# Additions in DRAM in four pieces each, and a fixed order of splits in the first channel block of a ConvFFN

## The chip, the cores and the metric

The kernel runs on one core of a Trainium2 chip. A core has a matrix engine (TensorE, PE in the profile, with its weight loads as PEld), three engines for elementwise work (VectorE or DVE, ScalarE or ACT, GpSimd or POOL), and SyncE (SP), which here only issues transfers. Transfers run on 16 DMA engines that all queues share; a queue of SP and a queue of POOL feed them in this kernel. The metric is the device time of one execution in microseconds (us). Before the change, three runs gave 1703.12, 1707.95 and 1720.14 us, so the median is 1707.95 us.

## What is computed

One layer of a diffusion backbone is applied to 128 context tokens and 1024 latent tokens of width 1024: a mixer of gated linear attention, then a channel mixer, each with a normalisation and a modulation before it and a gate behind it. The change lies in the channel mixer:

```python
def dw_conv(u, conv_w, conv_b, grid):
    # 3x3 over the latent grid (16 rows of 64), width 3 over the context tokens
    ...
    return out + conv_b

def conv_ffn(h, w_up, conv_w, conv_b, w_down, grid):
    u = dw_conv(h @ w_up, conv_w, conv_b, grid)
    gate, up = jnp.split(u, 2, axis=-1)
    return (jax.nn.silu(gate) * up) @ w_down

# in trunk_layer
h = rmsnorm(x, norm2) * (1 + scale2) + shift2
x = x + gate2 * conv_ffn(h, w_ffn_up, ffn_conv, b_ffn_conv, w_ffn_down, grid)
```

Everything is float32. `w_ffn_up` is 1024 x 5632 and `w_ffn_down` 2816 x 1024.

## The kernel before

**Products in float32.** PE multiplies a rounded form of float32 here. Each operand is therefore split into a high part, which ACT copies into the rounded type, and a low part, which DVE or POOL computes as the difference (`split_lo`, line 62). A product is three matmul passes: high x high, high x low, low x high.

**Seven products in place of eight.** The up projection and the down projection both use a Strassen-like scheme. Tokens and inner dimension are halved, sums and differences of the halves of both operands are formed, and seven products of half size replace eight. For the up projection the token operands are `b11`, `b21`, `b22`, straight from the normalised tokens, and the sums `t1` to `t4`; the weight operands are the blocks `11`, `12`, `21`, `22` of a channel's columns and the sums `s1` to `s4`. The 128 context tokens have an operand `p` of their own.

**The up stage.** It has 22 channel blocks (`c` from 0 to 21, called channels below) of 128 gate and 128 up columns. In channel `c` PE runs the products in an order that is written out (`chained`): for every channel but the first 5 (`t1`), the transposed context columns of the channel before (`prompt_columns`, line 1507), product 4 of the channel before (`t4`), 2 (`b21`), 3 (`b22`), 1 (`b11`), the context product's first half, 6 (`t2`), its second half, 7 (`t3`). Channel 0 begins with 1, 2, 5 and has 6, 3 and then both halves of the context product. DVE adds partial products (lines 1572, 1573, 1579) and runs the 3x3 convolution as eight multiply-adds over each half (`conv_rows`, line 1426), after ACT has written the middle tap (line 1414). The result of the gate half and of the up half are multiplied on POOL (line 1522) and stored to DRAM (`scr_g`, line 1523). Every second channel POOL forms four sums of stored values (`token_sums`, lines 1389 to 1393).

**Weights of the up stage.** SP loads the four blocks of the channel after next as rows 1 and 2, two loads of 256 KB each (`load_row`, line 1287). One buffer, `ra`, holds them, so a row can be loaded only when the split of the old row has read it. POOL forms the weight sums of the next channel (`weight_sums`, lines 1307 to 1310: s1 = 21 + 22, s2 = s1 - 11, s4 = 12 - s2, s3 = 11 - 21) and the low parts of all splits of weights (line 62), which PE needs a channel later. The split weights live in nine slots, so a split also waits until PE has used up the block whose slot it takes.

**Sums of `w_down`.** The down projection needs four sums of halves of `w_down`, `scr_t[0]` to `scr_t[3]`, in DRAM, each with 11 planes of 128 x 512. They are made by DMA alone, issued on POOL's queue: a copy of one half, and then a transfer that adds another half onto it. Eight transfers of 2816 KB stand in `sums_todo` (lines 1400 to 1407); `second_half(c)` issues one per channel from channel 1 on, behind the product of line 1522.

**The way into the up stage.** The last of three token groups is normalised, transposed by PE (line 1133) and modulated by DVE and ACT into `RAW` (the four raw token blocks, lines 1146 and 1150) and `raw_p`. Then come lines 1342 to 1362: the first weights are split, the sums of channels 0 and 1 are formed on POOL, and DVE and ACT form and split the token sums in two pieces of 256 columns (lines 1349 to 1355, 1157 and 62). A planner that follows program order and priorities places the instructions on each engine; `tc.issue_after(x)` fixes that what is in the block comes behind `x` on `x`'s engine, and `tc.high_priority()` moves work ahead. The first pieces were given high priority. `t1` lived in the pool `h2b`, whose space is in use by the stage before.

Of the kernel before, what the change touches and what calls it, by code (L numbers as in the profile page):

```python
# [8 lines left out]
F32 = mybir.dt.float32  # L9
F32R = mybir.dt.float32r  # L10
BF16 = mybir.dt.bfloat16
U8 = mybir.dt.uint8
AF = mybir.ActivationFunctionType
ALU = mybir.AluOpType
# [3 lines left out]
P = 128  # L18
D = 1024
NS = 1024  # L20
# [5 lines left out]
NPAIR = 11  # L26
# [20 lines left out]
def kernel(ctx: ExitStack, tc: tile.TileContext, ins, outs, stop=None):  # L47
    nc = tc.nc
    y_prompt, y_sample, new_gla, new_hgrn = outs

    def pool(stack, name, bufs, space=None, side=None):
        kw = {} if space is None else {"space": space}
        if side is not None:
            kw["side"] = side
        return stack.enter_context(tc.tile_pool(name=name, bufs=bufs, reuse_waits="tile", **kw))
# [3 lines left out]
    anchor = {}  # L59

    def split_lo(eng, out, full, hi):
        eng.tensor_tensor(out, full, hi.bitcast(F32), op=ALU.subtract)  # L62


    const = pool(ctx, "const", 1)
# [19 lines left out]
    scr_mod = {g: dram.tile([P, 512], F32, name=f"scr_mod{g}") for g in "BC"}  # L85
# [3 lines left out]
    scr_t = [dram.tile([NPAIR, P, 512], F32, name=f"scr_t{i}") for i in range(4)]  # L89
# [195 lines left out]
    modr = {}  # L285
# [266 lines left out]
    s2 = const.tile([P, KT, 2], F32, name="s2")  # L552
    b2 = const.tile([P, KT, 2], F32, name="b2")
    gate1, conv_c, last_head, w_late, again = {}, [], [], {}, {}
# [473 lines left out]
    for n, u in enumerate(groups):  # L1028
# [9 lines left out]
        for bi, b in enumerate(ORDER):  # L1038
            fb, k, k0 = ready
            lv = levels(u, b, fb, k, k0)  # L1040
            for slot in range(8):
                last = anchor["mm"] = next(lv)
# [9 lines left out]
                for part in range(2):  # L1052
# [3 lines left out]
                    while streamed < goal:  # L1056
                        with tc.issue_after(anchor["mm"].ins) if n == 5 else nullcontext():
                            got = next(steps, None)
# [10 lines left out]
    for n, _ in enumerate(chain(states, outs_)):  # L1069
        while streamed < cols_all + REST_COLS * (n + 1) / 13:  # L1070
            with tc.issue_after(anchor["mm"].ins):
                got = next(steps, None)
# [22 lines left out]
    es_h2 = ExitStack()  # L1095
    HB = {"h": {}, "l": {}}
    h2a = pool(es_h2, "h2a", 1, side="right")
    for nm in ("b11", "b21"):
# [3 lines left out]
    RAW = {  # L1102
        (i, j): h2a.tile([P, 4, 512], F32, name=f"rb{i}{j}", tag=f"r{i}{j}") for i in range(2) for j in range(2)
    }
    convc = conv_c[0]

    def gate_bc(stack_pool, g, js, v, nm, t=None):
# [46 lines left out]
    def split_h(nm, raw, eng, cs=slice(0, 512)):  # L1154

        hi, lo = HB["h"][nm][:, :, cs], HB["l"][nm][:, :, cs]
        nc.scalar.activation(hi, raw, AF.Copy)
        split_lo(eng, lo, raw, hi)


    w7 = w_late[7]
    for g in range(3):
# [29 lines left out]
        if g < 2:  # L1192
            l7 = lhs(7)
            for i in range(3):
                for n, (a, wi) in enumerate(((0, 0), (0, 1), (1, 0))):
                    for half in range(2):
                        cs = slice(half * 512, (half + 1) * 512)
                        mm(us[i][:, cs], l7[a][:, i * P : (i + 1) * P], w7[wi][:, cs], start=(n == 0), stop=(n == 2))
                done(i)
        else:  # L1200
            order = (1, 2, 0, 3, 4, 5, 6, 7)
# [33 lines left out]
    accs = [accp.tile([P, NT], F32, name=f"acc{i}") for i in range(4)]  # L1235
    p1_t = accp.tile([P, 512], F32, name="cp1")
    h2b = pool(es_h2, "h2b", 1, side="right")
    for nm in ("b22", "p", "t2", "t1"):
        for x in "lh":
            HB[x][nm] = h2b.tile([P, KT, P] if nm == "p" else [P, 4, 512], F32R, name=f"{nm}{x}")  # L1240
    gs = {}
# [50 lines left out]
    def split_slots(c, names, eng):  # L1292
        names = sorted_by_slot(c, names)
        ss = [SLOT[c][nm] for nm in names]
        t = ra if names[0][0] in "12" else sr
        first = {"11": 0, "12": 0, "21": 2, "22": 2, "s1": 0, "s4": 1, "s2": 1, "s3": 3}[names[0]]
        raw = flat(t[:, first : first + len(ss)])
        dims = [[1, 512]] if len(ss) == 1 else [[(ss[1] - ss[0]) * 512, 2], [1, 512]]
        hi, lo = (aps(flat(W[k]), ss[0] * 512, dims) for k in "hl")
        if len(ss) == 2:  # L1300
            raw = raw.rearrange("p (s n) -> p s n", s=2)
        nc.scalar.activation(hi, raw, AF.Copy)  # L1302
        split_lo(eng, lo, raw, hi)

    def weight_sums(c, eng):
        r = {nm: at(c, nm) for nm in SLOT[c]}
        eng.tensor_tensor(r["s1"], r["21"], r["22"], op=ALU.add)
        eng.tensor_tensor(r["s2"], r["s1"], r["11"], op=ALU.subtract)
        eng.tensor_tensor(r["s4"], r["12"], r["s2"], op=ALU.subtract)
        eng.tensor_tensor(r["s3"], r["11"], r["21"], op=ALU.subtract)  # L1310
# [20 lines left out]
    def rb(i, j, n):  # L1331
        return RAW[i, j][:, :, pieces[n]]
# [9 lines left out]
    split_slots(0, ("21", "22"), nc.gpsimd)  # L1342
    load_row(1, 1)
    load_row(1, 2)
    weight_sums(1, nc.gpsimd)
    tt = nc.vector.tensor_tensor
    for n, cs in enumerate(pieces):
        with tc.high_priority() if n == 0 else nullcontext():
            tt(tmp[n], rb(0, 1, n), rb(0, 0, n), op=ALU.subtract)
            tt(tmp[2 + n], rb(1, 1, n), tmp[n], op=ALU.subtract)  # L1350
            split_h("t1", tmp[n], nc.vector, cs)
            tt(tmp[n], rb(1, 0, n), tmp[2 + n], op=ALU.subtract)
            split_h("t2", tmp[2 + n], nc.vector, cs)
            split_h("b22", rb(1, 1, n), nc.vector, cs)
            tt(tmp[2 + n], rb(1, 1, n), rb(0, 1, n), op=ALU.subtract)
    for nm, i in (("t3", 0), ("t4", 1)):
        for x, j in (("h", 0), ("l", 1)):
            HB[x][nm] = h2a.tile([P, 4, 512], F32R, name=f"{nm}{x}", tag=f"r{i}{j}")
        for n, cs in enumerate(pieces):
            split_h(nm, tmp[2 + n if nm == "t3" else n], nc.vector, cs)  # L1360
    nc.scalar.activation(HB["h"]["p"], again["p"], AF.Copy)
    split_lo(nc.vector, HB["l"]["p"], again["p"], HB["h"]["p"])

    late = again["late"].tile([P, 2304], F32, name="late", tag="mh7")
    ss_t = late[:, 0:2048].rearrange("p (i n) -> p i n", i=4)
# [18 lines left out]
    def token_sums(j):  # L1384
# [8 lines left out]
        nc.gpsimd.dma_start(scr_s[j], t)  # L1393


    halves = [
        [w_down.rearrange("(j h p) f -> h j p f", h=2, p=P)[h][:, :, fs] for fs in (lo_f, hi_f)] for h in range(2)
    ]
    sums_todo = [
        lambda: nc.gpsimd.dma_start(scr_t[0], halves[0][1]),  # L1400
        lambda: nc.gpsimd.dma_start(scr_t[2], halves[1][1]),
        lambda: nc.gpsimd.dma_start(scr_t[0], halves[0][0], accum_op=ALU.add),
        lambda: nc.gpsimd.dma_start(scr_t[2], halves[0][1], accum_op=ALU.add),
        lambda: nc.gpsimd.dma_start(scr_t[1], scr_t[0]),
        lambda: nc.gpsimd.dma_start(scr_t[1], halves[1][1], accum_op=ALU.add),
        lambda: nc.gpsimd.dma_start(scr_t[3], scr_t[1]),
        lambda: nc.gpsimd.dma_start(scr_t[3], halves[1][0], accum_op=ALU.add),
    ]

    def conv_rows(u, ch, acc, ra=0, rb=NROW):  # L1410

# [69 lines left out]
    def up_prompt(c, half):  # L1481


        pk = pks[c]
        a, b = sorted(SLOT[c][f"{row}{half + 1}"] for row in (1, 2))

        def products():
            for kt in range(4):
                for n, (h, x) in enumerate((("h", "h"), ("h", "l"), ("l", "h"))):
                    last = mm(  # L1490
                        pk,
                        HB[h]["p"][:, 4 * half + kt, :],
                        aps(flat(W[x]), a * 512 + kt * P, [[(b - a) * 512, 2], [1, P]]),
                        start=(half + kt + n == 0),
                        stop=(half == 1 and kt == 3 and n == 2),
                        skip_group_check=True,
                    )
            return last

        chained(products)  # L1500
# [30 lines left out]
    for c in range(NHID + 1):  # L1531
        n = c + 1 if c + 1 < NHID else None
        if c < NHID:
            acc[c] = conv_tiles(c)
            u[c] = [ps_u.tile([P, NS], F32, name="u", tag="u")]

        if c == 0:
            u[0].append(ps_u.tile([P, NS], F32, name="u", tag="u"))
            anchor["pe"] = anchor["turned"]
            for p in (1, 2):  # L1540
                up(0, p)
        if c < NHID:
            up(c, 5)
        if c > 0:
            prompt_columns(c - 1)
            up(c - 1, 4)
            second_half(c - 1)
        if c == NHID:
            break
        if n:  # L1550
            split_slots(n, ("21", "22"), nc.gpsimd)
            if n + 1 < NHID:
                load_row(n + 1, 2)
        if c > 0:
            up(c, 2)
            up(c, 3)
            u[c].append(ps_u.tile([P, NS], F32, name="u", tag="u"))
            up(c, 1)
        pks[c] = ps_p.tile([P, 2 * P], F32, name="x", tag="x")
        if c > 0:  # L1560
            up_prompt(c, 0)
        up(c, 6)
        if c == 0:
            up(c, 3)
            up_prompt(c, 0)
        if n:
            split_slots(n, ("s1",), nc.gpsimd)
            split_slots(n, ("11", "12"), nc.gpsimd)
            if n + 1 < NHID:
                load_row(n + 1, 1)  # L1570
        F, S = u[c]
        nc.vector.tensor_tensor(F[:, 0:512], F[:, 0:512], copies["p1"], op=ALU.add)
        nc.vector.tensor_tensor(F[:, 512:NS], F[:, 512:NS], copies["u2"], op=ALU.add)
        up_prompt(c, 1)
        nc.scalar.activation(pt_t, pks[c], AF.Copy)
        if n:
            split_slots(n, ("s2", "s4"), nc.gpsimd)
        up(c, 7)
        nc.vector.tensor_tensor(S[:, 512:NS], S[:, 0:512], copies["p5"], op=ALU.add)
        anchor["conv"] = conv_rows(F, c, acc[c][0])  # L1580
        if n:
            split_slots(n, ("s3",), nc.gpsimd)
            if n + 1 < NHID:
                weight_sums(n + 1, nc.gpsimd)
# [127 lines left out]
    p1, u2, u3 = {}, {}, {}  # L1712
# [115 lines left out]
```

## Time and profile before

| what | number |
|---|---|
| runs | 1703.12, 1707.95, 1720.14 us |
| the execution that was profiled: its time | 1704.19 us |
| its span, from the first to the last instruction | 1702.4 us |
| mean granted TensorE clock | 0.972 of full speed |
| the up stage, from the first product to the last (line 1316) | 886.8 to about 1440 us |
| the largest transfers of the up stage, median from issue to landing | 27.0 us for six with 2816 KB each |

The profile names engines as above. A row of a group or of a timeline names the line of the kernel, the engine, the operation, the tiles (what is written, an arrow, what is read) and the shape; in brackets or behind a bar stands how long the engine sat idle before it and what ended that idle time. A row of waits reads: engine, tile and line that waited, what it waited for, microseconds in total, times, longest. SPq and POOLq are the transfers that these engines issue. Windows are counted in us from the start of the span.

### The profile page before, as it was taken

To read this page: it belongs to the slowest core of one execution; us is meant where nothing else is said; L and a number is where in the kernel's file an instruction comes from. 1 tells how busy PE (TensorE), PEld (TensorE's weight loads), DVE (VectorE), ACT (ScalarE), POOL (GpSimd) and SP (SyncE) were. 2 spreads that over 40 slices of the span, in tenths; PEclk is the share of its full clock that TensorE was granted. 3 is DMA by queue.
4 is the path that set the end of the run, shared out by engine and by line. 5 is a ranking of instruction groups with operands and counts; after the bars stand their busy time and mean duration, and the time that the engine had idled before them with its cause. 6 is when DMAs were issued, how large, how long until landed. Compare 5 with 4: busy or idle time off the path is not lost.

```text
span 1702.4 us, 23982 instructions
## 1 busy us (share of the span) xinstructions
PE 1599.4 (94%) x9050; PEld 1346.1 (79%) x9050; DVE 1189.7 (70%) x1720; ACT 752.5 (44%) x1397; POOL 712.5 (42%) x523
## 2 busy tenths in 40 slices
PE   7999998999999999899877998789999999999997
PEld 2788886998999999878656887567788887788886
DVE  4554456066576667854669997678899999777665
ACT  4443345253545344511664443333444444447444
POOL 2402012232423323111255987777999997300001
PEclk9999999999999999999978999899899999999999
DMA  9234343221322304253821357676222224679862
GB/s 353 78 95 124 116 132 106 74 90 50 111 64 69 115 32 157 77 230 139 306 99 38 115 183 170 190 188 157 98 94 102 96 97 147 253 259 338 284 193 117
DMA packets 166349, 244.18 MB, mean 143 GB/s; under 512 B 14132, under 2 KB 110626, under 8 KB 164186
## 3 DMA queue, kind: packets, MB, share of 16 engines
q1 hardware_dynamic: 142583, 168.54, 30.8%
q0 software_dynamic: 23040, 73.43, 13.1%
q8 instruction: 71, 1.16, 0.3%
q10 hardware_dynamic: 611, 0.68, 0.1%
q14 instruction: 44, 0.36, 0.1%
HBM read 186.95 MB, written 78.71 MB: 156 GB/s over the span
## 4 chain that ended last, share of the span: by engine, by line
PE 73%; DMA 9%; POOL 6%; DVE 6%; issue 4%; ACT 1%; SPq 0%; POOLq 0%; DVEq 0%; ACTq 0%
PE u L1316 16%; PE mm L580 15%; PE mm L594 6%; PE lv L862 5%; PE xb L1690 5%; PE yb L1690 5%; DMA ra<-in_w_ffn_up_dram 5%; PE mm L720 3%; PE x L1490 3%; POOL wul L62 2%; PE yb L1741 2%; PE u L1211 2%; PE mm L485 1%; PE x L903 1%; PE o L938 1%
## 5 line engine op out<-in xcount | busy, mean ns | idle before, releaser
L1426 DVE SCALAR_TENSOR_TENSOR acc<-u,convc,acc 128x945 f32<-128x945 f32 (+2 forms) x352 | 426.8, 1218 | 10.8 <-ACT acc L1414 4.4
L62 POOL TENSOR_TENSOR wl<-raw,wh 128x1024 fp32r<-128x1024 f32 x42 | 102.1, 2435 | 271.8 <-ACT wh L123 246.9
L580 PE MATMUL mm<-h1h,wh 128*128 128x384 f32 x528 | 184.7, 350 | 0.0
L580 PE MATMUL mm<-h1l,wh 128*128 128x384 f32 x528 | 180.9, 343 | 0.0
L580 PE MATMUL mm<-h1h,wl 128*128 128x384 f32 x528 | 180.9, 343 | 0.0
L862 PE MATMUL lv<-Q,m 64*128 64x128 f32 (+1 forms) x1008 | 126.6, 295 | 12.5 <-DVE Q L871 6.7
L879 DVE COPY_PREDICATED S<-masks,lv 128x384 f32<-128x384 uint8 x168 | 98.7, 587 | 54.5 <-PE lv L862 54.3
L62 POOL TENSOR_TENSOR wul<-sr,wuh 128x512 fp32r<-128x512 f32 (+1 forms) x68 | 121.9, 1793 | 33.5 <-ACT wuh L1302 33.1
L855 ACT ACTIVATE m<-k 128x384 f32<-128x384 f32 x126 | 69.8, 556 | 142.3 <-DVE k L873 119.2
L871 DVE TENSOR_TENSOR Q<-Q,fb 128x384 f32<-128x384 f32 x126 | 92.8, 736 | 54.7 <-PE lv L862 54.0
L862 PEld LDWEIGHTS lv<-Q,m 64*128 64x128 f32 (+1 forms) x1008 | 107.5, 190 | 26.6 <-issue 10.7
L62 POOL TENSOR_TENSOR wul<-ra,wuh 128x1024 fp32r<-128x1024 f32 x46 | 116.6, 2535 | 11.8 <-ACT wuh L1302 7.6
L580 PEld LDWEIGHTS mm<-h1h,wh 128*128 128x128 f32 x528 | 100.3, 190 | 5.5 <-issue 3.7
L580 PEld LDWEIGHTS mm<-h1l,wh 128*128 128x128 f32 x528 | 100.1, 190 | 1.5 <-issue 0.8
L1665 POOL TENSOR_TENSOR sq<-sq,mhalf 128x1 f32<-128x1 f32 x9 | 11.1, 1237 | 214.1 <-DVE sq L1662 214.1
L580 PEld LDWEIGHTS mm<-h1h,wl 128*128 128x128 f32 x528 | 99.9, 189 | 0.7 <-issue 0.6
L123 ACT ACTIVATE wh<-raw 128x1024 fp32r<-128x1024 f32 x55 | 58.1, 1058 | 62.3 <-DMA raw<-in_w_in_dram 22.8
L594 PE MATMUL mm<-wh,h1h 128*128 128x256 f32 x288 | 83.2, 289 | 0.0
L594 PE MATMUL mm<-wl,h1h 128*128 128x256 f32 x288 | 80.9, 281 | 0.0
L873 DVE TENSOR_TENSOR k<-k,fb 128x384 f32<-128x384 f32 x126 | 76.1, 608 | 6.7 <-ACT m L855 2.7
L594 PE MATMUL mm<-wh,h1l 128*128 128x256 f32 x288 | 80.8, 281 | 0.0
L1302 ACT ACTIVATE wuh<-ra 128x1024 fp32r<-128x1024 f32 x44 | 46.3, 1053 | 62.0 <-DMA ra<-in_w_ffn_up_dram 27.4
(346 smaller groups left out, 4478.9 us busy)
## 6 DMA issues: line engine op xcount, KB each, us to landing
ra<-in_w_ffn_up_dram SPq DMA_DIRECT2D x88, 256.0 KB, 3.1
scr_t<-in_w_ffn_down_dram POOLq DMA_DIRECT2D x6, 2816.0 KB, 27.0
raw<-in_w_in_dram SPq DMA_DIRECT2D x32, 512.0 KB, 4.5
raw<-in_w_ada_dram SPq DMA_DIRECT2D x32, 512.0 KB, 3.7
scr_g<-acc POOLq DMA_DIRECT2D x22, 576.0 KB, 4.0
scr_s<-late POOLq DMA_DIRECT2D x11, 1024.0 KB, 5.0
wa<-in_w_ada_dram SPq DMA_DIRECT2D x16, 512.0 KB, 6.1
raw<-in_w_out_dram SPq DMA_DIRECT2D x13, 512.0 KB, 10.0
```

What stands on the lines that cost most here:

```text
L62: eng.tensor_tensor(out, full, hi.bitcast(F32), op=ALU.subtract)
L123: nc.scalar.activation(hi, raw, AF.Copy)
L580: mm(ps, a[:, kt, :], h[kt][b], start=(n == 0), stop=(n == 23))
L594: mm(ps, h[kt][t // 3][:, ts_], a[:, kt % 4, :], start=(n == 0), stop=(n == 23))
L855: nc.scalar.activation(aps(kmix, 0, [[2 * h, NB], [h, 2], [1, h]]), aps(kf_, 0, [[2 * h, NB], [BL + h, 2], [1, h]]), AF.Copy)
L862: last = mm(ps[:, i, :], kmix[r0:r1, i * P : (i + 1) * P], aps(Qf_, i * P, dims, r0, r1), start=True, stop=True,)
L871: nc.vector.tensor_tensor(qm, qm, aps(ff_, 2 * h - 1, [[BL - h, 2], [2 * h, NB], [0, h]]), op=ALU.mult)
L873: nc.vector.tensor_tensor(km, km, aps(ff_, BL + 2 * h - 1, [[-(BL + h), 2], [2 * h, NB], [0, h]]), op=ALU.mult)
L879: nc.vector.copy_predicated(S_, masks[:, lev : lev + 1, :].to_broadcast([P, 3, P]), ps)
L1316: last = mm(dst, W[x][:, a, kt, :], HB[y][b][:, kt, :], start=(start and n == 0), stop=(stop and n == 11), skip_group_check=True,)
L1426: last = nc.vector.scalar_tensor_tensor(o, u3[:, r0 + dy : r1 + dy, c0 + dx : c1 + dx], wc(3 * (dy + 1) + dx + 1), o, op0=ALU.mult, op1=AL ...
L1690: anchor["down"] = mm(banks[i], w[a][:, ts_], w[b][:, 512:1024], start=(start and j == 0 and n == 0), stop=(j == NPAIR - 1 and n == 2), sk ...
```

## The change

The diff has three parts. First, a transfer that adds onto `scr_t[i]` is replaced by four that add 3, 3, 3 and 2 of the 11 planes; the copies stay whole. So 20 transfers instead of 8 are handed out, one per channel from channel 1. Second, the token sums and splits before and in channel 0 get a fixed order on DVE and ACT: each step made with `queued` comes behind the step before. The order is `t1`, `p`, `t2`, `b22`, `t3`; the two splits of `t4` come behind the additions of line 1573 in channel 0. The first half of the context product goes ahead of product 6 in channel 0. The sums of channel 1's weights go behind the split of its blocks 21 and 22, and the split of its s2 and s4 behind the convolution of channel 0's first half. Third, `t1` and the gate row `modr["B"]` get a pool of their own, `h2t`, opened before the stage that leads to the up stage, and the row is loaded when that pool is opened.

```diff
     def split_lo(eng, out, full, hi):
-        eng.tensor_tensor(out, full, hi.bitcast(F32), op=ALU.subtract)
+        return eng.tensor_tensor(out, full, hi.bitcast(F32), op=ALU.subtract)
...
+    h2t = pool(es_h2, "h2t", 1, side="right")
+    modr["B"] = h2t.tile([P, 512], F32, name="modrB", tag="t1h")
+    nc.sync.dma_start(modr["B"], scr_mod["B"])
...
-        nc.scalar.activation(hi, raw, AF.Copy)
-        split_lo(eng, lo, raw, hi)
+        first = nc.scalar.activation(hi, raw, AF.Copy)
+        return first, split_lo(eng, lo, raw, hi)
...
-    for nm in ("b22", "p", "t2", "t1"):
+    for x in "hl":
+        HB[x]["t1"] = h2t.tile([P, 4, 512], F32R, name=f"t1{x}", tag=f"t1{x}")
+    for nm in ("b22", "p", "t2"):
...
-    weight_sums(1, nc.gpsimd)
     tt = nc.vector.tensor_tensor
-    for n, cs in enumerate(pieces):
-        with tc.high_priority() if n == 0 else nullcontext():
-            tt(tmp[n], rb(0, 1, n), rb(0, 0, n), op=ALU.subtract)
-            tt(tmp[2 + n], rb(1, 1, n), tmp[n], op=ALU.subtract)
-            split_h("t1", tmp[n], nc.vector, cs)
-            tt(tmp[n], rb(1, 0, n), tmp[2 + n], op=ALU.subtract)
-            split_h("t2", tmp[2 + n], nc.vector, cs)
-            split_h("b22", rb(1, 1, n), nc.vector, cs)
-            tt(tmp[2 + n], rb(1, 1, n), rb(0, 1, n), op=ALU.subtract)
+    with tc.high_priority():
+        tt(tmp[0], rb(0, 1, 0), rb(0, 0, 0), op=ALU.subtract)
+        tt(tmp[2], rb(1, 1, 0), tmp[0], op=ALU.subtract)
+        split_h("t1", tmp[0], nc.vector, pieces[0])
+        tt(tmp[0], rb(1, 1, 0), rb(0, 1, 0), op=ALU.subtract)
+    order = {"dve": tt(tmp[1], rb(0, 1, 1), rb(0, 0, 1), op=ALU.subtract)}
+
+    def queued(fn):
+
+        with tc.issue_after(order["dve"].ins):
+            with tc.issue_after(order["act"].ins) if "act" in order else nullcontext():
+                got = fn()
+        if isinstance(got, tuple):
+            order.update(act=got[0], dve=got[1])
+        else:
+            order["dve"] = got
+
+    def parts(nm, raws):
+        for n, cs in enumerate(pieces):
+            queued(lambda: split_h(nm, raws[n], nc.vector, cs))
+
+    def split_prompt_tokens():
+        first = nc.scalar.activation(HB["h"]["p"], again["p"], AF.Copy)
+        return first, split_lo(nc.vector, HB["l"]["p"], again["p"], HB["h"]["p"])
+
+    queued(lambda: split_h("t1", tmp[1], nc.vector, pieces[1]))
+    queued(split_prompt_tokens)
+    queued(lambda: split_h("t2", tmp[2], nc.vector, pieces[0]))
+    queued(lambda: tt(tmp[3], rb(1, 1, 1), tmp[1], op=ALU.subtract))
+    queued(lambda: split_h("t2", tmp[3], nc.vector, pieces[1]))
+    parts("b22", [rb(1, 1, n) for n in range(2)])
+    queued(lambda: tt(tmp[1], rb(1, 1, 1), rb(0, 1, 1), op=ALU.subtract))
+    for n in range(2):
+        queued(lambda: tt(tmp[2 + n], rb(1, 0, n), tmp[2 + n], op=ALU.subtract))
...
-        for n, cs in enumerate(pieces):
-            split_h(nm, tmp[2 + n if nm == "t3" else n], nc.vector, cs)
-    nc.scalar.activation(HB["h"]["p"], again["p"], AF.Copy)
-    split_lo(nc.vector, HB["l"]["p"], again["p"], HB["h"]["p"])
+    parts("t3", tmp[0:2])
...
-    sums_todo = [
-        lambda: nc.gpsimd.dma_start(scr_t[0], halves[0][1]),
-        lambda: nc.gpsimd.dma_start(scr_t[2], halves[1][1]),
-        lambda: nc.gpsimd.dma_start(scr_t[0], halves[0][0], accum_op=ALU.add),
-        lambda: nc.gpsimd.dma_start(scr_t[2], halves[0][1], accum_op=ALU.add),
-        lambda: nc.gpsimd.dma_start(scr_t[1], scr_t[0]),
-        lambda: nc.gpsimd.dma_start(scr_t[1], halves[1][1], accum_op=ALU.add),
-        lambda: nc.gpsimd.dma_start(scr_t[3], scr_t[1]),
-        lambda: nc.gpsimd.dma_start(scr_t[3], halves[1][0], accum_op=ALU.add),
-    ]
+    sums_todo = []
+
+    def sum_copy(i, src):
+        sums_todo.append(lambda: nc.gpsimd.dma_start(scr_t[i], src))
+
+    def sum_add(i, src):
+        for j in range(0, NPAIR, 3):
+            js = slice(j, min(j + 3, NPAIR))
+            sums_todo.append(lambda js=js: nc.gpsimd.dma_start(scr_t[i][js], src[js], accum_op=ALU.add))
+
+    sum_copy(0, halves[0][1])
+    sum_copy(2, halves[1][1])
+    sum_add(0, halves[0][0])
+    sum_add(2, halves[0][1])
+    sum_copy(1, scr_t[0])
+    sum_add(1, halves[1][1])
+    sum_copy(3, scr_t[1])
+    sum_add(3, halves[1][0])
...
         if n:
-            split_slots(n, ("21", "22"), nc.gpsimd)
+            last = split_slots(n, ("21", "22"), nc.gpsimd)
+            if n == 1:
+                with tc.issue_after(last.ins):
+                    weight_sums(1, nc.gpsimd)
...
-        if c > 0:
-            up_prompt(c, 0)
+        up_prompt(c, 0)
         up(c, 6)
         if c == 0:
             up(c, 3)
-            up_prompt(c, 0)
...
-        nc.vector.tensor_tensor(F[:, 512:NS], F[:, 512:NS], copies["u2"], op=ALU.add)
+        last = nc.vector.tensor_tensor(F[:, 512:NS], F[:, 512:NS], copies["u2"], op=ALU.add)
+        if c == 0:
+            with tc.issue_after(last.ins):
+                parts("t4", tmp[2:4])
         up_prompt(c, 1)
         nc.scalar.activation(pt_t, pks[c], AF.Copy)
-        if n:
+        if c > 0 and n:
             split_slots(n, ("s2", "s4"), nc.gpsimd)
         up(c, 7)
         nc.vector.tensor_tensor(S[:, 512:NS], S[:, 0:512], copies["p5"], op=ALU.add)
         anchor["conv"] = conv_rows(F, c, acc[c][0])
+        if c == 0:
+            split_slots(n, ("s2", "s4"), nc.gpsimd)
```

More of the change, by code (lines that the diff above doesn't have):

```diff
@@ L1302, in split_slots @@
         nc.scalar.activation(hi, raw, AF.Copy)
-        split_lo(eng, lo, raw, hi)
+        return split_lo(eng, lo, raw, hi)
     def weight_sums(c, eng):
```

## The prediction

> **What bounds the kernel now.** The views were read in this order: the page's head and slices, the busy time by stretches, the waits of PE and POOL in those stretches, the DMA issues in the stretch of one addition, and then the timelines of POOL and DVE.
>
> ```profile
> span 1702.4 us, 23982 instructions
> PE 1599.4 (94%) x9050; PEld 1346.1 (79%) x9050; DVE 1189.7 (70%) x1720; ACT 752.5 (44%) x1397; POOL 712.5 (42%) x523
> ...
> 921.00:1034.40 113.40, 113.40 (x551) 93.51 (x550) 109.03 (x115) 53.58 (x71) 98.82 (x64) 1.00 0.46 138
> 1034.40:1214.20 179.80, 150.57 (x661) 121.13 (x660) 131.19 (x139) 63.17 (x84) 135.45 (x90) 0.89 0.65 170
> 1214.20:1418.20 204.00, 204.00 (x991) 168.05 (x990) 196.60 (x207) 94.16 (x126) 184.21 (x120) 1.00 0.28 95
> ```
>
> The three rows of stretches are the up stage, cut where a channel's transposed prompt columns (line 1507) begin; a row gives length, then busy time of PE, PEld, DVE, ACT, POOL, then granted clock, share of the DMA engines and GB/s. The first holds 5 channels, 113.40/5 = 22.68 us each; the third 9, 204.00/9 = 22.67 us each; PE fills both. The middle one holds 6 channels and takes 179.80 us, where 6 x 22.67 = 136.0 would do: **43.8 us too much**, with PE busy 150.57 us and a clock of 0.89. This is what can be had there.
>
> ```profile
> PE u L1316 <- POOL wul L62: 21.3, 4, 8.2
> PE u L1316 <- DVE acc L1426: 8.0, 3, 3.0
> ...
> POOL sr L1307 <- DMA ra<-in_w_ffn_up_dram: 44.1, 4, 11.9
> POOL wul L62 <- ACT wuh L1302: 1.5, 3, 0.7
> ...
> scr_t<-in_w_ffn_down_dram POOLq DMA_DIRECT2D x1, 2816.0 KB, 27.4
> ra<-in_w_ffn_up_dram SPq DMA_DIRECT2D x4, 256.0 KB, 11.3
> ...
> ra<-in_w_ffn_up_dram SPq DMA_DIRECT2D x88, 256.0 KB, 3.1
> ...
> 1015.58 1.91 POOL L1402 DMA_DIRECT2D scr_t<-in_w_ffn_down_dram  x1
> ...
> 1021.11 3.16 POOL L62 TENSOR_TENSOR wul<-ra,wuh 128x1024 fp32r<-128x1024 f32 x1
> ...
> 1029.75 3.11 POOL L62 TENSOR_TENSOR wul<-ra,wuh 128x1024 fp32r<-128x1024 f32 x1
> 1042.10 1.27 POOL L1307 TENSOR_TENSOR sr<-ra 128x512 f32<-128x512 f32 x1 [9.25 <-DMA ra<-in_w_ffn_up_dram]
> ```
>
> In the middle stretch PE waits 21.3 us for POOL's low parts and, as their echo, 8.0 us for DVE; the rest of the 43.8 is slow clock after each stall. POOL itself waits 44.1 us, 4 times, at line 1307 for the next channel's weight rows. The DMA rows of 1010 to 1046 us say why: one whole addition takes 27.4 us to land, and a 256 KB weight load beside it 11.3 us, where the median over the kernel is 3.1. The load of row 2 is issued when the split at 1021.11 has read the old row, 8 us into the addition; POOL needs it at about 1032.9 and has it at 1042.1. There are four such waits, and four additions.
>
> **The change part by part.** (1) *Additions in pieces.* Four transfers of 11 planes become sixteen of 3, 3, 3 and 2 planes. By planes of the row above a piece lasts 27.4 x 3/11 = 7.5 us; with a start that does not shrink (the small early packets, some 2 to 3 us) an estimate is 9 us. So a piece is all but over when row 2's load is issued 8 us after it, and row 1's load follows later still.
>
> ```profile
> POOL sr L1307 <- DMA ra<-in_w_ffn_up_dram: 3.1, 2, 2.8
> POOL wul L62 <- ACT wuh L1302: 1.3, 1, 1.3
> ...
> scr_t<-in_w_ffn_down_dram POOLq DMA_DIRECT2D x1, 2816.0 KB, 15.3
> ...
> L1403 POOL DMA_DIRECT2D scr_t<-in_w_ffn_down_dram x1: 1981/1981/1981, 1048.8 to 1048.8; - x1
> L1404 POOL DMA_DIRECT2D scr_t<-scr_t x1: 557/557/557, 1081.4 to 1081.4; - x1
> L1407 POOL DMA_DIRECT2D scr_t<-in_w_ffn_down_dram x1: 2012/2012/2012, 1160.4 to 1160.4; - x1
> ...
> POOL wul L62 <- ACT wuh L1302: 17.6, 6, 3.5
> POOL scr_s L1393 <- POOL late L1392: 1.6, 4, 0.7
> ...
> L120 SPq DMA_DIRECT2D raw<-scr_t x16: 320/430/1347, 1486.6 to 1627.8; - x16
> ```
>
> The nearest row is the pair of plain copies of whole halves between 960 and 1012 us, where one lands in 15.3 us: POOL waited 3.1 us in both together, at most 2.8, and PE not at all. A piece is shorter than that copy, so its wait lies between 0 and 2.8 us; I take 0, since 9 is far under 15.3. What a piece costs POOL to issue is between 0.56 (the contiguous copy, line 1404) and 2.01 (a whole addition, line 1407). By planes, 0.56 + (1.98 - 0.56) x 3/11 = 0.95 us. The cover is POOL's idle time in the quiet stretch: 17.6 + 1.6 = 19.2 us over 9 channels, 2.1 each. So 0.95 is hidden, 2.01 just so; what exceeds 2.1 is paid each time, 16 times. Part 1 takes away 43.8 us, against a worst case of 16 x (2.01 + 2.8 - 2.1) = 43.
>
> The twenty transfers now fill channels 1 to 20, where the eight ended in channel 8. All four stalls go with the long additions; next in line is PE itself, full in both quiet stretches, and close behind it DVE, 196.60 of 204.00 us. A channel's store, behind the piece on POOL's queue, waits 9 us there instead of 27. The last piece is issued a whole channel, some 24 us from a channel's columns to its store, after the end of the quiet stretch: at 1418.2 + 24 = 1442 on this trace's clock, while the sums are first read at 1486.6, and the fourth, which it completes, in the second to last set of products. So nothing waits for it, and the tail keeps its length; without that cover it would cost one piece, 9 us.
>
> (2) *Order in channel 0.*
>
> ```profile
> PE u L1316 <- DVE t1l L62: 8.8, 1, 8.8
> ...
> 879.34 0.54 DVE L1150 TENSOR_SCALAR rb<-x,s,b 128x256 f32<-128x256 f32 x1 [4.40 <-PE x L1133]
> ...
> 887.28 2.07 DVE L62 TENSOR_TENSOR t1l<-acc,t1h 128x1024 fp32r<-128x1024 f32 x1
> 889.28 2.33 DVE L62 TENSOR_TENSOR t2l<-acc,t2h 128x1024 fp32r<-128x1024 f32 x1
> ...
> 902.60 1.21 DVE L62 TENSOR_TENSOR b22l<-rb,b22h 128x1024 fp32r<-128x1024 f32 x1
> ...
> 911.76 2.35 DVE L62 TENSOR_TENSOR t4l<-acc,t4h 128x1024 fp32r<-128x1024 f32 x2
> 914.03 1.21 DVE L62 TENSOR_TENSOR t3l<-acc,t3h 128x1024 fp32r<-128x1024 f32 x1
> ...
> 917.94 1.20 DVE L1426 SCALAR_TENSOR_TENSOR acc<-u,convc,acc 128x945 f32<-128x945 f32 x1 [1.28 <-ACT acc L1414]
> ...
> 888.23 2.29 POOL L1307 TENSOR_TENSOR sr<-ra 128x512 f32<-128x512 f32 x1
> ...
> 908.10 2.66 POOL L62 TENSOR_TENSOR wul<-ra,wuh 128x1024 fp32r<-128x1024 f32 x1 [7.65 <-ACT wuh L1302]
> 915.00 1.41 POOL L62 TENSOR_TENSOR wul<-sr,wuh 128x512 fp32r<-128x512 f32 x1 [4.24 <-ACT wuh L1302]
> ...
> 915.45 0.39 PE L1316 MATMUL u<-t3h,wuh 128*128 128x512 f32 x1
> ...
> 918.24 0.40 PE L1316 MATMUL u<-t1h,wuh 128*128 128x512 f32 x1
> ```
>
> PE stands 8.8 us at the fifth product until both pieces of t1l are there. The change moves the second piece ahead of t2 and b22, gives t1 memory of its own (so that its first piece can fill DVE's idle 4.40 us before 879.34), and holds channel 1's weight sums on POOL behind the split at 908.10. That stall should go. But DVE works without a break from 887.28 to 915.24, and PE's seventh product starts at 915.45, just when t3l is done: what is late next is the whole DVE list. A 128x1024 subtraction takes 1.21 us alone (902.60) and 2.07 to 2.33 while POOL adds (888.23, 2.29 where such an add takes 1.27): the two take turns. The sums moved off 888 land among t3 and t4, so the turns are paid later, not saved. Count: the first t1 piece goes into idle time, about 2.1 us; the two t4 pieces, 2.35 us, leave the list before t3 but stand before the first convolution (917.94), which has to end before PE gets its next buffer; and new waits come in: the prompt's split, now second in a fixed order, cannot start before the last modulated column, about 2 us, and t2's second piece waits for its copy on ACT, about 1. Gain 2 to 4, loss 3: I take **0**, with the ends -8.8 (all of the stall) and +5 (both t4 pieces and both waits on the path).
>
> [...]
>
> The rest of (2) at nothing: the sums of channel 1, four of 1.27 us, go where POOL idles 4.24 us before 915.00; 4 x 1.27 - 4.24 = 0.8, which pushes the split of s1 from its end at 916.4 to 917.2, and PE wants it at 918.24; without that second it would cost up to 0.8. The prompt's product is the same matmuls in another place. The split of s2 and s4 goes behind the start of the convolution, an instruction of about 1.2 us, and the product that wants it is the fourth from 918.24; without that cover it costs those 1.2.
>
> (3) *The gate row.*
>
> ```profile
> 806.71 0.32 SPq L1110 DMA_DIRECT2D modrB<-scr_modB  x1
> 807.20 7.04 SPq L1177 DMA_DIRECT2D xt<-scr_pre  x5
> ```
>
> The load of the gate row goes ahead on SP's queue; it takes 0.32 us and stands already in front of these loads. If its new place frees later, the loads behind it are late by that: between -0.3 us (its own issue) and +7 (the 7.04 of the loads behind it), taken as 0, for it reuses space of the same closed stage.
>
> Sum: 1704.19 (the execution profiled; its span is 1702.4) - 43.8 + 0 + 0 = 1660.4 us. The median of the runs, 1707.95, lies 3.8 above the profiled execution, so I round up to **1661**.
>
> **The rivals.** *The pieces still press on POOL*: each waits as the copies did and issues dear. Half of 3.1 us is 1.55; with 0.95 that is 2.5, 0.4 over the cover: 16 x 0.4 = 6 us, 1667. At the upper ends 43 are lost, 1703; in the middle 1685. For it: POOL is busy 184.21 of 204.00 us in the quiet stretch. Against it: two whole copies in a row did not stop PE.
>
> [...]
>
> *The t1 stall goes as well*, nothing being late next: 1660.4 - 8.8 = 1651.6. Against it: the unbroken DVE list.
>
> *Slower*: a piece delays row 2's load as a whole addition does, by 44.1/4 = 11.0 us, because the load still meets it in the engines. Then 16 x (11.0 + 0.95 - 2.1) = 158 replace 43.8: 1818. It decides from 43.8/16 + 2.1 = 4.8 us of issue and wait per piece. Against it: the 2.8 us of the longer copies.
>
> *The change does not do what it says*: the stalls were DMA traffic in sum, only spread out: about 1700. Against it: the engines are busy 0.46 in the first stretch, with two copies, and PE is full.
>
> **How the numbers follow.** Forecast 0.62 (1655 to 1666), t1 stall gone too 0.14, POOL pressed 0.16 (1666 to 1703), only spread 0.04, slower 0.04. The range of 1650 to 1678 holds the first two and over half of the third. About 1% (17 us) is what a measurement of this kernel can tell from no change. Faster by more needs under 1691: 0.62 + 0.14 + 0.15 = 0.91; same 0.06; slower 0.03.
>
> **What would show it.** Right: no stretch of channels over 22.7 us each; no wait of PE for POOL; no wait at line 1307 of over 3 us; sixteen issues of about 1 us, landing in 7 to 11. For part 2: no wait for t1l, a new one for t3l, b22l or the convolution. Wrong: waits at 1307 in most channels, or POOL busy without a break and PE behind it.

## The result, and the profile after

The changed kernel takes 1808.52 us (median of 4 runs, 1800.64 to 1815.70). The kernel before, with a fourth run of 1705.41 us, has a median of 1706.68. The ratio is 1.058, with a 95% interval of 1.0507 to 1.0653: the change makes the kernel slower by some 100 us, where 43 us less were forecast. The execution profiled took 1807.15 us, its span is 1805.4 us.

The stretches of the kernel after are cut at the same events as those below of the kernel before: the first up product, the transposed columns (line 1507 before, 1543 after) of channels 1, 20 and 21, and the end. Between the columns of channels 1 and 20 lie 19 channel lengths, 430.8 us at 22.67 us each. The columns are length, busy time of PE, PEld, DVE, ACT and POOL, granted clock, share of the DMA engines, GB/s.

```profile
0.00:893.10 893.10, 839.24 (x5566) 725.99 (x5567) 516.02 (x1015) 381.11 (x918) 224.92 (x209) 0.97 0.37 124
893.10:950.10 57.00, 49.23 (x220) 39.35 (x219) 55.25 (x44) 29.62 (x37) 44.44 (x23) 0.92 0.16 47
950.10:1503.50 553.40, 471.72 (x2091) 380.25 (x2090) 414.38 (x438) 200.28 (x266) 415.24 (x272) 0.90 0.40 112
1503.50:1531.80 28.30, 22.82 (x100) 18.30 (x99) 19.82 (x21) 9.47 (x13) 20.03 (x13) 0.88 0.64 173
1531.80:1805.40 273.60, 252.57 (x1079) 203.53 (x1077) 183.80 (x205) 133.52 (x164) 34.27 (x22) 0.97 0.68 233
```

The same five stretches of the kernel before:

```profile
0.00:886.80 886.80, 835.25 (x5567) 723.35 (x5567) 515.62 (x1013) 381.34 (x918) 224.14 (x210) 0.98 0.38 125
886.80:943.70 56.90, 48.12 (x220) 39.38 (x219) 54.27 (x46) 29.39 (x37) 39.83 (x22) 0.89 0.14 42
943.70:1418.30 474.60, 445.37 (x2092) 363.95 (x2091) 415.29 (x437) 199.17 (x266) 400.92 (x263) 0.96 0.47 136
1418.30:1438.40 20.10, 20.10 (x99) 16.48 (x98) 18.90 (x20) 9.44 (x13) 14.88 (x11) 1.00 0.50 168
1438.40:1702.40 264.00, 250.57 (x1079) 202.97 (x1077) 185.64 (x205) 133.16 (x164) 32.69 (x21) 0.99 0.68 238
```

Length against length, the 103.0 us of difference are 6.3 before the up stage, 0.1 on the way into it (57.00 against 56.90), **78.8 in the 19 channel lengths**, 8.2 in the next one and 9.6 from there to the end. DVE, ACT and PE have the same work in the long stretch; PE is slow or idle. What PE and POOL wait for in that stretch (us in total, times, longest):

```profile
PE u L1322 <- POOL wul L62: 65.8, 13, 8.0
PE u L1322 <- DVE acc L1462: 15.9, 6, 3.2
...
POOL sr L1313 <- DMA ra<-in_w_ffn_up_dram: 129.8, 15, 11.6
```

The chain is the one of before: PE waits for low parts of POOL, with an echo on DVE, and POOL waits at the weight sums (line 1313 now) for the weight rows. Thirteen of the 15 last 8.7 to 11.6 us, where the kernel before has four of 9.3 to 11.9; the other two are under 1 us. The DMA issues between 900 and 1425 us, with count, size and median time to landing:

```profile
ra<-in_w_ffn_up_dram SPq DMA_DIRECT2D x72, 256.0 KB, 10.3
scr_g<-acc POOLq DMA_DIRECT2D x16, 576.0 KB, 24.9
...
scr_t<-in_w_ffn_down_dram POOLq DMA_DIRECT2D x9, 768.0 KB, 27.3
...
scr_t<-in_w_ffn_down_dram POOLq DMA_DIRECT2D x3, 512.0 KB, 27.1
```

A weight load takes 10.3 us and a channel's store, queued behind a piece, 24.9. The last two rows hold the surprise: a piece of 768 KB lands after 27.3 us and one of 512 KB after 27.1, and a whole addition of 2816 KB took 27.4. **Cutting the transfers did not shorten them.** The timeline of POOL shows one piece and its wait:

```profile
1184.15 1.93 POOL L1435 DMA_DIRECT2D scr_t<-in_w_ffn_down_dram  x1
...
1189.68 3.18 POOL L62 TENSOR_TENSOR wul<-ra,wuh 128x1024 fp32r<-128x1024 f32 x1
...
1210.55 1.27 POOL L1313 TENSOR_TENSOR sr<-ra 128x512 f32<-128x512 f32 x1 [11.59 <-DMA ra<-in_w_ffn_up_dram]
```

The distances are those of a whole addition: the row is freed 8 us in, and the wait is 11.59 us where it was 9.25 to 11.9. Why the time does not shrink shows in the DMA engines. POOL's queue in 10 us in the middle of a whole addition (before, 1030 to 1040 us) and in the middle of a piece (after, 1068 to 1078):

```profile
q0 software_dynamic: 569, 1.17, 62.6%
```

```profile
q0 software_dynamic: 154, 0.32, 16.9%
```

The columns are packets, MB and the share of the time of 16 engines. 62.6% of 16 is 10.0 engines at work, 16.9% is 2.7. A whole addition has 11 planes as its outermost dimension, a piece 3: it looks as if each plane went to one engine, and a piece used 3 engines for as long as the whole used 11.

How three busy engines can hold up a weight load shows a little later in the same piece, from 1074 to 1077 us. Two weight loads were issued at 1069.6 and 1070.0, and POOL waits for a weight row until 1080.3:

```profile
q0 software_dynamic: 46, 0.09, 16.9%
q1 hardware_dynamic: 45, 0.02, 3.8%
```

`q1` is SP's queue. Both queues together keep only 3.3 of the 16 engines at work (20.7%), and SP's packets go one for one with POOL's. So what is left of the loads appears to sit on the three engines of the piece and to take turns with it, while the others have nothing to do; the view does not name the engines.

### The profile page after: what moved, and what is told of

Same layout as the page of the kernel before. It is cut to its first block, busy times and chain, and to the rows that moved or that the text cites. A ratio compares the mean times of both kernels' runs of the same rounds, so it can differ in the third digit from the quotient of the medians.

```text
span 1805.4 us, 24012 instructions
## 1 busy us (share of the span) xinstructions
PE 1635.6 (91%) x9050; PEld 1367.4 (76%) x9050; DVE 1189.3 (66%) x1720; ACT 754.0 (42%) x1397; POOL 738.9 (41%) x535
## 4 chain that ended last, share of the span: by engine, by line
PE 59%; DMA 17%; POOL 12%; DVE 6%; issue 4%; ACT 1%; SPq 1%; POOLq 0%; DVEq 0%; ACTq 0%
PE mm L580 15%; DMA ra<-in_w_ffn_up_dram 12%; PE mm L594 6%; POOL wul L62 5%; PE u L1322 5%; PE lv L862 5%; PE xb L1732 5%; PE yb L1732 5%; PE mm L720 3%; PE yb L1783 2%; PE u L1215 2%; DMA scr_g<-acc 2%; PE o L938 1%; PE x L903 1%; PE mm L485 1%
## 5 line engine op out<-in xcount | busy, mean ns | idle before, releaser
L62 POOL TENSOR_TENSOR wul<-sr,wuh 128x512 fp32r<-128x512 f32 (+1 forms) x68 | 134.4, 1978 | 11.4 <-ACT wuh L1308 11.1
L62 POOL TENSOR_TENSOR wul<-ra,wuh 128x1024 fp32r<-128x1024 f32 x46 | 128.3, 2788 | 13.3 <-ACT wuh L123 7.2
L1322 PE MATMUL u<-b22h,wul 128*128 128x512 f32 x88 | 47.3, 537 | 65.8 <-POOL wul L62 65.8
L1479 DVE SCALAR_TENSOR_TENSOR acc<-x,convc,acc 128x127 f32<-128x127 f32 x88 | 30.3, 344 | 108.2 <-ACT acc L1475 108.2
L1313 POOL TENSOR_TENSOR sr<-ra 128x512 f32<-128x512 f32 x22 | 30.8, 1402 | 132.4 <-DMA ra<-in_w_ffn_up_dram 129.8
## 6 DMA issues: line engine op xcount, KB each, us to landing
ra<-in_w_ffn_up_dram SPq DMA_DIRECT2D x88, 256.0 KB, 10.3
scr_g<-acc POOLq DMA_DIRECT2D x22, 576.0 KB, 24.9
scr_t<-in_w_ffn_down_dram POOLq DMA_DIRECT2D x12, 768.0 KB, 27.3
```

Of the source, the lines that this page charges most:

```text
L62: return eng.tensor_tensor(out, full, hi.bitcast(F32), op=ALU.subtract)
L1322: last = mm(dst, W[x][:, a, kt, :], HB[y][b][:, kt, :], start=(start and n == 0), stop=(stop and n == 11), skip_group_check=True,)
```

## The experiments

Theory A says just that: a transfer is spread over as many DMA engines as its outermost dimension counts. Theory B: an adding transfer has a fixed time. Theory C: the order in channel 0 is to blame. The first four runs share their chip.

**The pieces alone.** The kernel before, with `sums_todo` built as in the diff of the change, and nothing else of it.

```diff
-        lambda: nc.gpsimd.dma_start(scr_t[0], halves[0][0], accum_op=ALU.add),
...
+            sums_todo.append(lambda js=js: nc.gpsimd.dma_start(scr_t[i][js], src[js], accum_op=ALU.add))
```

> The kernel before with the additions in pieces, nothing else changed. Theory A (planes): a transfer is spread over as many DMA engines as its outermost dimension counts, so a whole addition runs on 11 engines and a piece of 3 planes on 3, each engine still moving one plane; a piece then lands after about 27 us like the whole addition, and sixteen additions stall POOL at the weight sums in place of four. Theory B (fixed): an adding transfer takes some 27 us whatever its size or shape. Both: 1790 to 1810 us, landing near 27 us. Theory C (order): the loss comes from the fixed order in channel 0, which leaves DVE late for good, and the pieces are harmless: about 1660 us.

Measured: 1806.55 us, ratio 1.0563 (1.0512 to 1.0614); pieces land after 27.0 us. The pieces carry the whole loss, so C falls.

**The order alone.**

```diff
-    sum_add(0, halves[0][0])
...
+        lambda: nc.gpsimd.dma_start(scr_t[0], halves[0][0], accum_op=ALU.add),
```

> The changed kernel with the four additions whole again. A and B: 1700 to 1712 us, the same as before, since the first channel gains and loses about nothing, with four stalls of POOL at the weight sums, 44 us in all. C: 1790 us or more.

Measured: 1709.79 us, ratio 1.0009 (0.9982 to 1.0036); POOL waits 43.9 us in four waits at the sums. The fixed order, the moved gate row and `t1`'s own pool are worth nothing that can be measured.

**The same pieces, rows outermost.**

```diff
     def sum_add(i, src):
+        dst, src = (t.rearrange("j p f -> p j f") for t in (scr_t[i], src))
         for j in range(0, NPAIR, 3):
             js = slice(j, min(j + 3, NPAIR))
-            sums_todo.append(lambda js=js: nc.gpsimd.dma_start(scr_t[i][js], src[js], accum_op=ALU.add))
+            sums_todo.append(lambda js=js: nc.gpsimd.dma_start(dst[:, js], src[:, js], accum_op=ALU.add))
```

> The changed kernel with the same pieces of 3, 3, 3 and 2 planes, but each transfer written with its 128 rows as the outermost dimension and the planes behind it. Bytes, 2 KB runs and number of transfers stay the same. A: the rows spread over all 16 engines, a piece lands in 6 to 10 us, the stalls go, 1655 to 1672 us. B: landing stays near 27 us and the time near 1805.

Measured: 1665.25 us, ratio 0.9751 (0.9694 to 0.9808). The same bytes to the same places, in another order of dimensions, are worth 143 us against the changed kernel. The 19 channel lengths of this run, then its DMA issues from 900 to 1430 us, then POOL's issues of the pieces (ns, shortest, median, longest):

```profile
943.30:1374.20 430.90, 430.90 (x2092) 354.79 (x2091) 415.12 (x437) 198.90 (x266) 411.90 (x273) 1.00 0.52 146
```

```profile
ra<-in_w_ffn_up_dram SPq DMA_DIRECT2D x80, 256.0 KB, 3.0
...
scr_t<-in_w_ffn_down_dram POOLq DMA_DIRECT2D x12, 768.0 KB, 8.2
...
scr_t<-in_w_ffn_down_dram POOLq DMA_DIRECT2D x4, 512.0 KB, 5.9
```

```profile
L1436 POOL DMA_DIRECT2D scr_t<-in_w_ffn_down_dram x16: 1159/1304/1764, 1015.3 to 1396.5; - x16
```

PE is busy for all of 430.90 us, 22.68 for each of the 19. A piece lands after 8.2 us, and the weight loads are back at 3.0.

**Pieces of 32 rows of all planes**, planes outermost as before.

```diff
-        for j in range(0, NPAIR, 3):
-            js = slice(j, min(j + 3, NPAIR))
-            sums_todo.append(lambda js=js: nc.gpsimd.dma_start(scr_t[i][js], src[js], accum_op=ALU.add))
+        for p in range(0, P, 32):
+            ps = slice(p, p + 32)
+            sums_todo.append(lambda ps=ps: nc.gpsimd.dma_start(scr_t[i][:, ps], src[:, ps], accum_op=ALU.add))
```

> The changed kernel with each addition cut into four pieces of 32 rows of all 11 planes, planes outermost. A: 11 engines as in a whole addition, each with a quarter of the work, landing 27/4 = 7 us and a start of 2 to 3, so 9 to 10 us; 1655 to 1675 us. B: landing near 27 us, time near 1805.

Measured: 1666.71 us, ratio 0.9751 (0.9696 to 0.9807), landing:

```profile
scr_t<-in_w_ffn_down_dram POOLq DMA_DIRECT2D x16, 704.0 KB, 9.3
```

B falls with both: transfers of the same kind and nearly the same size land after 27, 9 and 8 us.

**Whole additions, rows outermost.** The next four runs share a chip, and all start from the kernel before.

```diff
     def sum_add(i, src):
         dst, src = (t.rearrange("j p f -> p j f") for t in (scr_t[i], src))
-        for j in range(0, NPAIR, 3):
...
+        sums_todo.append(lambda: nc.gpsimd.dma_start(dst, src, accum_op=ALU.add))
```

> The kernel before, its four additions whole, but with the 128 rows as the outermost dimension. From the four landings seen so far (27.2 us for 128 runs of 2 KB per engine, 9.3 for 32, 8.2 for 24, 5.9 for 16) a line of 3.35 us and 0.186 us per run comes out. Theory A (engines by the outermost dimension): 16 engines, 88 runs each, landing 3.35 + 16.4 = 19.7 us; the row load still meets it, POOL waits some 6 us four times where it waited 11, and 15 to 30 of the 43.8 us come back: 1675 to 1692. Theory B2 (the number of transfers is what counts, a whole addition cannot be made shorter): landing 27 and about 1708.

Measured: 1694.77 us, ratio 0.9903 (0.9868 to 0.9937); a little over the range of 1675 to 1692. Landing and POOL's wait at the sums between 940 and 1390 us:

```profile
scr_t<-in_w_ffn_down_dram POOLq DMA_DIRECT2D x6, 2816.0 KB, 20.0
```

```profile
POOL sr L1307 <- DMA ra<-in_w_ffn_up_dram: 20.9, 4, 7.9
POOL sr L1307 <- PE u L1316: 10.9, 2, 8.2
```

The landing of 20.0 us is the median of four additions and two copies; the additions alone land after 20.0 to 20.4, close to the 19.7 worked out. The first row holds the waits at three additions, 5.1, 7.4 and 7.9 us, and one of 0.5 ahead of them. The wait at the fourth addition is the 8.2 us that the list puts down to PE. Together the four are 28.6 us where they were 44.1, 7.1 each and not 6. More engines shortened an addition, to 20.0 us from 27.4, but only quarters spread as widely, at 8.2 and 9.3, were out of the way.

**No additions.** The copies stay, the additions are left out.

```diff
-    sum_add(0, halves[0][0])
-    sum_add(2, halves[0][1])
...
```

> The kernel before without its four additions (the four copies stay); the sums of halves are left out, so the down projection works on copies of halves. This is the floor for what the additions cost: 1704 - 44 = 1660 us by the channels' stretches; 1655 to 1668. If the pieces of rows still cost something, this is faster than the run with pieces spread over the rows (1665) by it.

Measured: 1666.79 us, ratio 0.9736 (0.9694 to 0.9778). This is the floor, and the run with spread pieces stands on it: its additions cost nothing that can be measured.

**Spread pieces without the order.** The edit of the rows-outermost run, on the kernel before.

```diff
+        dst, src = (t.rearrange("j p f -> p j f") for t in (scr_t[i], src))
...
+            sums_todo.append(lambda js=js: nc.gpsimd.dma_start(dst[:, js], src[:, js], accum_op=ALU.add))
```

> The kernel before with pieces of 3, 3, 3 and 2 planes, rows outermost, and nothing of the fixed order. If the fixed order is worth nothing, as the run with whole additions and the order showed (1.0009), this equals the run with both: 1660 to 1670 us. If the order was worth something that the stalls hid, this is slower than 1665 by it, up to 9 us.

Measured: 1664.82 us, ratio 0.9725 (0.9662 to 0.9788). The pieces alone do it: this kernel, with the smaller edit, is faster than the kernel before and than the changed one.

**Pieces of half planes.**

```diff
+        for js in (slice(0, 6), slice(6, NPAIR)):
+            for ps in (slice(0, 64), slice(64, P)):
+                sums_todo.append(
+                    lambda js=js, ps=ps: nc.gpsimd.dma_start(scr_t[i][js, ps], src[js, ps], accum_op=ALU.add)
+                )
```

> The kernel before with each addition in four pieces that have the bytes of the changed kernel's within 10%, but as 64 rows of 6 or of 5 planes, planes outermost. A: 6 or 5 engines, 64 runs each: landing 3.35 + 64 x 0.186 = 15.3 us, between the 27 of 3 planes and the 8 of 16 engines; the row load, issued 8 us in, is late by 1 to 3 us, most of it inside POOL's idle time: 1660 to 1685. If the bytes of a piece set the landing, it is 8 us; if an addition has a fixed time, 27 us and 1800.

Measured: 1689.71 us, ratio 0.9872 (0.9824 to 0.9919), 5 us over the range. Landing of the pieces of 6 and of 5 planes, and the waits at the sums:

```profile
scr_t<-in_w_ffn_down_dram POOLq DMA_DIRECT2D x8, 768.0 KB, 14.6
...
scr_t<-in_w_ffn_down_dram POOLq DMA_DIRECT2D x8, 640.0 KB, 14.6
```

```profile
POOL sr L1307 <- DMA ra<-in_w_ffn_up_dram: 17.8, 8, 3.7
```

768 and 640 KB land after the same 14.6 us: what counts is the 64 rows that each engine has. POOL's queue in the middle of a piece of 6 planes (1052 to 1056 us) and of one of 5 planes (1075 to 1079):

```profile
q0 software_dynamic: 148, 0.30, 42.0%
```

```profile
q0 software_dynamic: 127, 0.26, 35.3%
```

That is 6.7 and 5.6 engines at work. A piece of 2 planes in the changed kernel shows 12.4%, 2.0 engines (1128 to 1138 us), and a piece with rows outermost 102.4%, all 16 (1042 to 1045 us of that run). The view adds up the times of packets, so it counts engines only nearly. The store that waits behind a piece on the same queue is sharper. It has 128 packets of 4.5 KB, one per row, and while a piece of 11, 6, 5, 3 or 2 planes runs, in most cases just 40, 80, 88, 104 or 112 of them go through: 8 for each engine that the piece leaves free under theory A.

In the order of runs of 2 KB per engine under theory A the median landings are 5.9 us (16), 8.2 (24), 9.3 (32), 14.6 (64), 20.0 (88) and 26.8 to 27.3 (128, whether the transfer has 11, 3 or 2 planes). Five of the waits are 3.1 to 3.7 us, in every second channel, a little over the 1 to 3 expected; three are under 1 us. Profile against profile of the run with spread pieces and no order, the 19 channel lengths are 14.6 us longer and the rest up to the end 5.3; the expectation had put in nothing for the end.

**What binds the way into the up stage.** Two kernels were run once each, both the changed kernel with spread pieces; the times are those of their traces, from the first up product on. In the first one the four weight sums of channel 1 are left out.

```diff
-            if n == 1:
-                with tc.issue_after(last.ins):
-                    weight_sums(1, nc.gpsimd)
```

> The changed kernel with pieces of rows outermost, and without the four weight sums of channel 1 on POOL; that channel's s1 to s4 are then left out (old values are used). Measured from the start of the first up product to the transposed columns of channel 0, and to those of channel 1, which took 34.3 and 56.9 us in the kernel before, 32.5 and 57.0 in the changed one, 33.1 and 57.0 in its version with rows outermost. Theory T (turns): DVE's subtractions and POOL's sums take turns, so without four sums of 1.27 us DVE's list ends 5 us sooner: the wait of 5.7 us for t3 falls to 0 to 1.5, about 28 us to channel 0's columns, and, the first convolution following sooner too, 52 to 54 to channel 1's. Rival W (waits): the fixed order's own waits for ACT and the last modulated columns hold DVE back, the sums are beside the point: 32 to 33 and 56 to 57 us, wait for t3 still 5 us.

Measured: 31.8 us to channel 0's columns, 55.7 to channel 1's, and a wait of 4.6 us for t3. By the numbers the rival had it. But POOL had moved its next splits and sums into the gap, and DVE still met work there (its t4 sums took 5.66 us), so this run could not tell the two apart. In the second one POOL's work for channels 1 and 2 is left out as well.

```diff
-        return split_lo(eng, lo, raw, hi)
+        return nc.scalar.activation(lo, raw, AF.Copy) if c == 1 else split_lo(eng, lo, raw, hi)
...
-            if n + 1 < NHID:
+            if 1 < n < NHID - 1:
                 weight_sums(n + 1, nc.gpsimd)
```

> The kernel of the run before, in which POOL moved its next work forward into the place of the four sums, so that DVE still met it; now POOL has nothing to do for channels 1 and 2 while DVE works off its list: the sums of channels 1 and 2 are left out, and the low parts of channel 1's weights are copies of the whole weights, made by ACT. Theory T (turns): DVE's two t4 sums take 2.5 us where they took 5.7, its two t3 parts 2.4 where 3.4 to 4.5; the wait of PE for t3 is 0 to 1.5 us, 27 to 29 us pass from the first product to channel 0's columns and 50 to 53 to channel 1's. Rival W (the order's own waits): wait for t3 still 4 to 5 us, 31 to 33 and 55 to 57 us.

Measured: 25.1 us to channel 0's columns and 51.5 to channel 1's. DVE's t4 sums in the changed kernel, then in this one, and what PE waited for here:

```profile
908.14 5.67 DVE L1385 TENSOR_TENSOR acc<-rb,acc 128x1024 f32<-128x1024 f32 x2
```

```profile
911.86 2.35 DVE L1385 TENSOR_TENSOR acc<-rb,acc 128x1024 f32<-128x1024 f32 x2
```

```profile
PE u L1322 <- DVE acc L1463: 1.8, 1, 1.8
...
PE u L1322 <- DVE t3l L62: 0.2, 1, 0.2
```

The wait for t3 is gone with POOL's work, so turns it is, on one execution. The 25.1 us lie under the 27 to 29 of theory T, which had left out the clock: up to channel 0's columns the granted clock is 0.96 where it was 0.87 in the changed kernel, and PE is busy 24.21 us where it was 26.08. The convolution (line 1463) is next in line, as the prediction said.

## Why the prediction was wrong

*What bounds the kernel before* was read rightly: 43.8 us lay in four stalls that the additions cause. Without additions the kernel ran at 0.9736, and with short ones at 0.9725 and 0.9751, near the 1660.4 / 1704.19 = 0.9743 worked out.

*The step that failed* is the first of part 1: "By planes of the row above a piece lasts 27.4 x 3/11 = 7.5 us". I shared out the time of a transfer by its bytes, as if the 16 engines worked on it in turn. The runs show the planes side by side, about one engine each, so that fewer planes had fewer engines and the same 27 us: 10.0 engines at work and 27.4 us for 11 planes, 2.7 and 27.3 for 3. Three busy engines then held up a weight load as eleven did, 10.3 us to landing against 11.3; that its last part waits on just these engines is read from the 3.3 engines at work, not seen engine by engine.

Theory A rests on three readings. 11, 3 and 2 planes of 128 rows land after the same 26.8 to 27.3 us, 6 and 5 planes of half the rows after 14.6, three planes with 128 rows outermost after 8.2. The engines at work are 10.0, 6.7, 5.6, 2.7 and 2.0 for 11, 6, 5, 3 and 2 planes. And of the 128 packets of the store behind each, in most cases 40, 80, 88, 104 and 112 go through beside it. No addition with an outermost dimension between 11 and 128 was run, so how such a number is spread is not shown.

*The nearest row* that I leaned on, the plain copies, had 11 planes on the outside, as the whole additions have and the pieces do not. It bounded a transfer of another shape, and its 2.8 us was no upper end for a piece's wait.

*The rival "Slower"* came about in its mechanism: 1818 us were forecast for it, 1808.52 measured. Its size is in part luck. It had 16 waits, 158 us in all. The 19 channel lengths have 13 long ones, 9.9 us in the mean, and are 122.6 us over the 430.8 of a full PE; the last three pieces meet no weight row that POOL waits for. Another 17.8 us come from the tail, which the rival did not have. It had a chance of 0.04, on the strength of those copies. The rival "only spread" (DMA traffic in sum) falls: with rows outermost the same bytes move, and PE is full.

*The issue on POOL* was taken as 0.95 us by planes and is 1.94:

```profile
L1435 POOL DMA_DIRECT2D scr_t<-in_w_ffn_down_dram x16: 1902/1942/2678, 1021.7 to 1534.0; - x16
```

It did not shrink with the size either. Spread over rows it is 1.30 us, and that much was hidden, as the prediction said of all up to 2.1.

*The tail* did not keep its length: what follows the columns of channel 20 lost 17.8 us. The step holds for short pieces: with spread pieces this part takes 284.1 us, as in the kernel before. The chain of waits of the kernel after shows channel 20's store stuck behind the last piece, and a wait of PE that follows from it, since SP's queue waits for that store until 1566.5 us and issues the load of `modrC` at 1572.0:

```profile
1533.97 1.96 POOL scr_t L1435
1535.93 1.52 POOL wul L62
1537.45 29.02 DMA scr_g<-acc
```

```profile
PE yb L1663 <- DMA modrC<-scr_modC: 5.8, 1, 5.8
```

*Part 2 at 0* was right, and its working fits: the wait for t1l went and one of 5.7 us for t3l came, the columns of channel 0 stood 1.8 us sooner after the first product, those of channel 1 within 0.1 us of before. *Part 3 at 0* fits too: the gate row's load stands in the same place between the same loads, and the order alone made no difference. The 6.3 us ahead of the up stage are not the change's: the first up product came after 886.3 to 904.0 us in the profiles with the order and after 886.8 to 901.7 in those without it.

## What to carry to other kernels

A row's time can be shared out by its size only if the smaller piece runs on the same engines: here 3 of 11 planes took 27.3 us where all of them took 27.4. For a transfer, look first at its outermost dimension and at the share of the DMA engines while it runs. An addition like these is better cut along an inner dimension (32 rows of all 11 planes landed after 9.3 us) or written with a long one outermost (3 planes with 128 rows outermost, 8.2 us), so that each piece is still spread wide. When a bound is taken from the nearest row, ask whether that row has the shape of the new thing and not only a larger size.

## What had not been expected of the hardware

The additions from DRAM onto DRAM went in runs of 2 KB (1.17 MB in 569 packets from 1030 to 1040 us of the kernel before), and the median landings fit 3.35 us and 0.186 us for each run that one engine has under theory A, within 0.7 us; the two that were worked out ahead, 19.7 and 15.3 us, came out at 20.0 and 14.6. Pieces that kept about three engines out of 16 busy (2.7 by the view) were enough to raise the median landing of a 256 KB weight load from 3.1 to 10.3 us. And the issue of an addition by POOL followed its shape more than its bytes: a median of 1.94 us for the pieces of 3 and 2 planes, 1.30 for the same bytes with rows outermost, and 1.91 to 2.01 for all 11 planes.
